# Three more pairs of dilated tiles as block products, and the places of the combinations handed on one by one

## The chip, the cores and the metric

The kernel runs on one core of one Trainium2 chip. The metric is the time of one execution on the device in microseconds (us); the runs of the kernel before are given by their median. The engines are called as in the profile: PE is TensorE (PEld its weight loads), DVE is VectorE, ACT is ScalarE, POOL is GpSimd, SP is SyncE. Each of them works through its own queue in order and waits on semaphores for the others; DMAs are issued from the queues of SP, ACT and POOL.

## The reference

One layer of a decoder on a sequence of 1024 tokens of width 1024, all in float32. Two kinds of attention run on the same normalised input, are gated and summed, and an FFN follows:

```python
h = rms_norm(x, norm_mix_g)
proj = h @ w_in                    # columns: dilated q, k, v (3 x 768), fox q, k, v (3 x 512), 8 fgt, 2 x 1024 gates
dil = proj[..., :o2].reshape(b, s, 3, 3, 4, 64)      # 3 groups of 4 heads
f_logit = proj[..., o3:o4] + b_fgt
gates = sigmoid(proj[..., o4:] + b_gate)
for g, (window, dilation) in enumerate(((128, 1), (512, 4), (2048, 16))):
    o_g, lse_g = dilated_window_attention(q_g, k_g, v_g, window, dilation, slopes[g])
o_a = sum over g of softmax(lse)_g * o_g
o_b = forgetting_attention(fox q, k, v, log_sigmoid(f_logit))   # causal, 8 heads, decay by the cumulated log f
x = x + (g_a * (o_a @ w_dil_out) + g_b * (o_b @ w_fox_out)) @ w_out
gu = rms_norm(x, norm_ffn_g) @ w_ffn_in
x = x + (silu(gu[..., :DFF]) * gu[..., DFF:]) @ w_ffn_down       # DFF = 2816
out = rms_norm(x, norm_final_g)
```

## The kernel before

Every float32 matrix is split into two float32r parts, hi (ACT, L96) and lo (DVE, L97), and a product is three matmuls, hi x hi, hi x lo, lo x hi (mm3, L100 to L102). h lies transposed in SBUF as hT, 128 partitions by 8 slices of the contraction by 1024 tokens. A "tile" below is 128 columns of w_in, so 128 rows of the transposed projection.

The order of the kernel is: norm and transposes, fox values; dilated values; the combinations T1 to T4 of h (form); projections of fox q and k and of some of the dilated q and k as block products; the attention, fox first and dilated behind it; the merges of both with their gates; w_out; the FFN. The order on each engine is found by a scheduler that runs a model of the machine when the kernel is built. It puts work without a near deadline in the gaps of other work.

There are two ways to project a tile, and the change is about them.

- ahead() computes one tile with 2 halves x 8 slices x 3 = 48 matmuls into two banks of PSUM of a pool of its own (psf, tiles pf). ACT evacuates each half into fst and issues its store. These calls are the fillers of the attention: the list BESIDE (eight dilated tiles) and, behind it in the text, sixteen tiles of the gates (GATE0).
- projections() computes a pair of tiles as a 2 x 2 block product with 7 products instead of 8 (prod, 4 slices x 3 = 12 matmuls each, 84 together). For that it needs sums of the blocks of h, T1 to T4, which live in SBUF, and sums of the blocks of the weights, which POOL makes for each pair (left_side, tiles s12 and s34). The banks are evacuated by copy (ACT) and join (DVE). Four pairs are fox q and k, and the two pairs of TWOS are dilated.

The outputs of a pair are two tiles qo of 128 x 1024, which POOL's queue stores whole once both halves are there; the fox ones (hl=True) go as hi and lo.

T1 to T4 lie in one tile of 64 KB per partition, in the pool comb1, which is closed after the last pair. The pools of the attention (beside with fst and the bias tables R0, R1, R2; attention with q, k, scores and values) are opened behind it over the same memory. Behind the attention, both are closed, and the pool gates of the merges lies over their memory: load_o loads the attention's output from DRAM into land, and splits it into oh and ol.

fox_qk loads q and k of a pair of heads from DRAM: kx (L570), qx (L570) and ql (L571), five DMAs for each of two heads, on ACT's queue. fox_scores makes the scores (L588 and L589), masks on POOL, takes the maximum over keys on DVE and then across partitions on POOL (partition_all_reduce, L603). fox_exp subtracts and exponentiates, fox_values multiplies by the values vf (L639), with the denominators in L642. finish divides. For the dilated heads dil_scores and dil_values do the same (L351, L778, L781).

Of the kernel before, what the change touches and what calls it, by code (L numbers as in the profile page):

```python
# [15 lines left out]
P = 128  # L16
# [31 lines left out]
def layer_kernel(  # L48
# [166 lines left out]

    def ahead(pool, c0, dst, dl=1, sc=1.0):
# [7 lines left out]
        for hh in range(2):  # L224
            st = pool.tile([P, dl, n], F32, tag="fst", name=nm("fst"), bufs=2)
            nc.scalar.activation(out=st[:], in_=view(pf[hh][:], dl), func=AF.Copy, scale=sc)  # L226
            nc.scalar.dma_start(out=dst.rearrange("p (r i) -> p r i", r=dl)[:, :, hh * n:(hh + 1) * n], in_=st[:])
# [5 lines left out]
    TWOS = [[(0, g, a) for g in range(2)] for a in range(2)]  # L233
    BESIDE = [(0, 2, 0), (0, 2, 1)] + [(1, g, a) for g in range(3) for a in range(2)]
# [19 lines left out]
    def left_side(pool, rg, ru, bufs):  # L254
# [9 lines left out]
        S34, A22, A1 = pair(KT, "s34", 1), pair(4, "a22", bufs), pair_of(rg[:])  # L264
# [16 lines left out]
    def projections(pool, T, c, dst, dls, sc, hl=False):  # L281

        T1, T2, T3, T4 = T
        o1, o2 = [pool.tile([P, dl, S // dl], F32, tag="qo", name=nm("qo"), bufs=3) for dl in dls]
        n1, n2 = [HALF // dl for dl in dls]
# [20 lines left out]
        copy(o1[:, :, :n1], b1, dls[0])  # L306
# [8 lines left out]
        for o, d in zip((o2, o1), dst[::-1]):  # L315
            flat = o[:].rearrange("p r i -> p (r i)")
            if hl:
                hi = pool.tile([P, S], F32R, tag="qh", name=nm("qh"), bufs=1)
                split(hi[:], flat, flat)
                nc.gpsimd.dma_start(out=d[0], in_=hi[:].bitcast(F32))  # L320
                nc.gpsimd.dma_start(out=d[1], in_=flat)
            else:
                nc.gpsimd.dma_start(out=d, in_=flat)
# [93 lines left out]
    with pool_of("comb1", 1) as tpool:  # L417
        hl = tpool.tile([P, 2, 4, 4, HALF], F32R, name="tT1")
        T1, T2, T3, T4 = T = [Pair(hl[:, 0, i], hl[:, 1, i]) for i in range(4)]

        def form(k0):
            ks = slice(k0, k0 + 2)
            f1, f2, f3, f4 = [wpool.tile([P, 2, HALF], F32, tag=t, name=nm("f"), bufs=2)
                              for t in ("wh", "wh", "wl", "wl")]

            def vec(out, p, q, op=ALU.subtract):
                nc.vector.tensor_tensor(out=out[:], in0=p[:], in1=q[:], op=op)

            def back(out, b):

                vec(out, b.hi[:, ks].bitcast(F32), b.lo[:, ks].bitcast(F32), ALU.add)

            def keep(t, f):
                split(t.hi[:, ks], t.lo[:, ks], f[:])

            back(f3, B11)
            back(f2, B12)
            back(f4, B22)
            vec(f1, f2, f3)
            keep(T1, f1)  # L440
            vec(f2, f4, f2)
            keep(T3, f2)
            vec(f4, f4, f1)
            keep(T2, f4)
            back(f3, B21)
            vec(f3, f3, f4)
            keep(T4, f3)
# [3 lines left out]
        with pool_of("dilv", 1) as vpool:  # L451
            sts = [vpool.tile([P, 512], F32, name=nm("vst"), bufs=1) for _ in range(2)]
            w12 = Pair(*[vpool.tile([P, KT, 512], F32R, name=nm("wv"), bufs=1) for _ in range(2)])
            last = load_wv(w12, [(2 * DIL_W + 256 + i * P, P, i * P) for i in range(4)])
# [15 lines left out]
            with tc.issue_after(last.ins):  # L470
                form(0)
                form(2)
# [628 lines left out]
```

## Time and profile before

| what | value |
|---|---|
| median of 3 runs | 1529.3 us (1529.08 to 1530.83) |
| the profiled execution | 1531.32 us, span 1529.5 us |
| PE busy | 1477.5 us, 97% |
| DVE busy | 888.2 us, 58% |
| ACT busy | 527.9 us, 35% |
| POOL busy | 410.9 us, 27% |
| mean granted clock of PE | 0.991 |
| HBM | 116 GB/s over the span |

The span runs from the first to the last instruction of the profiled execution. A row of instructions gives its start and its length in us, the engine (ACTq is a DMA issue on ACT's queue), the line of the kernel, the operation, output<-input, shapes and count; in square brackets stands how long the engine sat idle before it and what ended that. A row of waits reads "who <- for whom: us in total, times, longest". A row of a stretch of time gives its length and then, per engine, busy time and count, and behind them the granted clock of PE as a share of full speed, the busy share of the DMA engines and GB/s. A row of DMAs gives the queue, the count, KB of each and the median time from issue to landing.

### The profile page before, as it was taken

The page shows a single profiled execution, that of the slowest core. Times are in us where ns is not written, and L with a number is a line of the kernel's source. Part 1 is how long each engine was busy: PE and PEld are TensorE (multiplying, and loading weights), DVE is VectorE, ACT ScalarE, POOL GpSimd, SP SyncE. Part 2 cuts the span into 40 slices and gives each one's busy share as a digit, 9 for nine tenths or more (in the row PEclk, how much of TensorE's full clock was granted, in tenths as well). Part 3 has the DMA queues.
Part 4 walks back from the last instruction along what each step waited for, and adds up shares of the span by engine and source line. Part 5 has one row for each costly group of instructions (what it writes and reads, how often), then busy time and mean ns, then how long its engine had stood idle before and what let it go on. Part 6 is the DMA issues. An engine that isn't in the chain of part 4 may idle for free.

```text
span 1529.5 us, 18174 instructions
## 1 busy us (share of the span) xinstructions
PE 1477.5 (97%) x6956; PEld 1194.4 (78%) x6956; DVE 888.2 (58%) x1313; ACT 527.9 (35%) x800; POOL 410.9 (27%) x361
## 2 busy tenths in 40 slices
PE   7999999899999999989999999999999999999997
PEld 6898878676766676878888788888888877788886
DVE  6482544289899998126726863444444445956546
ACT  5242322266554332235414332222222224312113
POOL 1002232254332211000000055555555553140000
PEclk9999999999999999999999999999999999999999
DMA  8132434755443612436713122222222225642202
GB/s 255 46 93 62 135 127 152 213 130 132 117 110 126 220 49 83 145 107 189 268 55 138 42 69 83 84 83 83 83 83 83 83 91 188 202 152 83 96 15 96
DMA packets 154055, 177.92 MB, mean 116 GB/s; under 512 B 17904, under 2 KB 120304, under 8 KB 153968
## 3 DMA queue, kind: packets, MB, share of 16 engines
q1 hardware_dynamic: 115536, 97.56, 21.5%
q10 hardware_dynamic: 27632, 40.38, 8.7%
q0 software_dynamic: 10800, 38.81, 6.8%
q8 instruction: 55, 0.90, 0.2%
q14 instruction: 32, 0.26, 0.1%
HBM read 125.35 MB, written 51.38 MB: 116 GB/s over the span
## 4 chain that ended last, share of the span: by engine, by line
PE 77%; DVE 8%; DMA 6%; ACT 4%; POOL 3%; issue 2%; ACTq 0%; SPq 0%; DVEq 0%; POOLq 0%
PE pd L278 23%; PE pd L100 10%; PE pd L102 10%; PE pd L101 10%; PE pf L100 5%; PE pf L101 4%; PE pf L102 4%; DMA wr<-in_w_ffn_in_dram 3%; ACT wh L96 2%; PE pd L190 2%; PE pd L191 2%; PE pd L194 2%; DVE wl L97 2%; POOL sg L1009 1%; PE pd L639 1%
## 5 line engine op out<-in xcount | busy, mean ns | idle before, releaser
L97 DVE TENSOR_TENSOR wl<-wr,wh 128x1024 fp32r<-128x1024 f32 (+2 forms) x152 | 165.4, 1091 | 189.3 <-ACT wh L96 185.6
L96 ACT ACTIVATE wh<-wr 128x1024 fp32r<-128x1024 f32 (+2 forms) x152 | 140.8, 932 | 360.7 <-PE pd L101 89.3
L278 PE MATMUL pd<-hT_t,wh 128*128 128x512 f32 x784 | 242.0, 390 | 1.4 <-ACT cc L291 0.7
L278 PE MATMUL pd<-tT,wh 128*128 128x512 f32 x672 | 206.9, 392 | 2.1 <-ACT wh L96 1.5
L278 PEld LDWEIGHTS pd<-hT_t,wh 128*128 128x128 f32 x784 | 147.0, 188 | 32.3 <-ACT cc L291 1.1
L100 PE MATMUL pf<-hT_t,wh 128*128 128x512 f32 x384 | 153.1, 399 | 5.8 <-ACT fst L226 5.8
L278 PE MATMUL pd<-hT_t,wl 128*128 128x512 f32 x392 | 154.0, 393 | 1.7 <-DVE wl L97 1.4
L101 PE MATMUL pf<-hT_t,wh 128*128 128x512 f32 x384 | 152.9, 398 | 0.0
L102 PE MATMUL pf<-hT_t,wl 128*128 128x512 f32 x384 | 152.5, 397 | 0.0
L278 PEld LDWEIGHTS pd<-tT,wh 128*128 128x128 f32 x672 | 126.6, 189 | 30.0 <-ACT wh L96 2.9
L100 PE MATMUL pd<-wh,wh 128*128 128x512 f32 x352 | 137.3, 391 | 3.6 <-DVE acc L1052 2.3
L101 PE MATMUL pd<-wl,wh 128*128 128x512 f32 x352 | 137.0, 389 | 0.0
L102 PE MATMUL pd<-wh,wl 128*128 128x512 f32 x352 | 137.0, 389 | 0.0
L278 PE MATMUL pd<-tT,wl 128*128 128x512 f32 x336 | 130.7, 392 | 2.4 <-DVE wl L97 2.3
L266 POOL TENSOR_TENSOR s<-wr 128x512 f32<-128x512 f32 x26 | 37.6, 1446 | 339.4 <-DVE tT L97 195.6
L1052 DVE TENSOR_TENSOR acc<-pd,acc 128x512 f32<-128x512 f32 x128 | 85.4, 685 | 67.3 <-PE pd L102 67.2
L97 DVE TENSOR_TENSOR wl<-s,wh 128x1024 fp32r<-128x1024 f32 x52 | 67.0, 1289 | 63.8 <-ACT wh L96 60.8
L96 ACT ACTIVATE wh<-s 128x1024 fp32r<-128x1024 f32 x52 | 55.0, 1060 | 117.5 <-POOL s L267 93.7
L100 PEld LDWEIGHTS pf<-hT_t,wh 128*128 128x128 f32 x384 | 73.6, 192 | 25.1 <-ACT fst L226 6.6
L278 PEld LDWEIGHTS pd<-hT_t,wl 128*128 128x128 f32 x392 | 73.6, 188 | 22.5 <-DVE wl L97 7.4
L101 PEld LDWEIGHTS pf<-hT_t,wh 128*128 128x128 f32 x384 | 73.6, 192 | 18.4 <-issue 3.5
L102 PEld LDWEIGHTS pf<-hT_t,wl 128*128 128x128 f32 x384 | 73.2, 191 | 17.0 <-issue 1.8
(243 smaller groups left out, 2751.1 us busy)
## 6 DMA issues: line engine op xcount, KB each, us to landing
wr<-in_w_in_dram SPq DMA_DIRECT2D x46, 512.0 KB, 4.3
wr<-in_w_ffn_in_dram SPq DMA_DIRECT2D x44, 512.0 KB, 4.5
wr<-a_dram SPq DMA_DIRECT2D x22, 512.0 KB, 4.3
wr<-in_w_ffn_down_dram SPq DMA_DIRECT2D x22, 512.0 KB, 3.7
a_dram<-a POOLq DMA_DIRECT2D x20, 512.0 KB, 5.0
g_dram<-fst ACTq DMA_DIRECT2D x32, 256.0 KB, 2.1
land<-g_dram SPq DMA_DIRECT2D x16, 512.0 KB, 3.6
dqk<-dqk_dram ACTq DMA_DIRECT2D x12, 512.0 KB, 5.7
```

What stands on the lines that cost most here:

```text
L96: nc.scalar.activation(out=hi, in_=src, func=AF.Copy)
L97: return nc.vector.tensor_tensor(out=lo, in0=src, in1=hi.bitcast(F32), op=ALU.subtract)
L100: nc.tensor.matmul(psum, w.hi, m.hi, start=start, stop=False)
L101: nc.tensor.matmul(psum, w.hi, m.lo, start=False, stop=False)
L102: last_mm[0] = nc.tensor.matmul(psum, w.lo, m.hi, start=False, stop=stop)
L190: nc.tensor.matmul(pt[hh][:], w.hi[:, k], m.hi, start=(k == 0), stop=False)
L191: nc.tensor.matmul(pt[hh][:], w.hi[:, k], m.lo, start=False, stop=False)
L194: nc.tensor.matmul(pt[hh][:], w.lo[:, k], m.hi, start=False, stop=(k == kt - 1))
L266: nc.gpsimd.tensor_tensor(out=s12[:, :4], in0=u1, in1=u2, op=ALU.add)
L278: last_mm[0] = nc.tensor.matmul(bank[:], p, q, start=first and k == 0 and n == 0, stop=k == 3 and n == 2, skip_group_check=True)
L639: nc.tensor.matmul(po[half[e], HALF - width[j]:], vf[:, j, pr, e], L[:, off[j]:off[j + 1]], start=(j == nj - 1), stop=(j == 0), skip_group ...
L1052: nc.vector.tensor_tensor(out=acc[:, t, cs], in0=pt[:], in1=acc[:, t, cs], op=ALU.add)
```

## The change

1. TWOS gets three more pairs: tiles (u, g, a), with u the pair of heads, g the group, a = 0 for q and 1 for k. BESIDE shrinks from eight tiles to two.
2. projections() writes each half of an output tile as soon as it is evacuated (put), from four small qo tiles; stores of the dilated halves go to runs of 1024 / stride / 2 elements. For fox, the high halves are stored from ACT's queue.
3. T1 to T4 become eight tiles of 8 KB, place(0) to place(7), whose pool stays open through the attention. The attention puts its q, k, maxima, values and dilated score tiles into them, each free once the products that read it are done.
4. The loads of q and k of the first pair of heads go to POOL's queue instead of ACT's. The tables R0 to R2 and the clearing of ql's lower half follow these loads in the text; the clearing moves from POOL to DVE.
5. The pool beside is on the right side of SBUF and is closed only behind the merges.

The core of the diff:

```diff
-    TWOS = [[(0, g, a) for g in range(2)] for a in range(2)]
-    BESIDE = [(0, 2, 0), (0, 2, 1)] + [(1, g, a) for g in range(3) for a in range(2)]
+    TWOS = [[(0, g, a) for g in range(2)] for a in range(2)] + [[(0, 2, a), (1, 0, a)] for a in range(2)]
+    TWOS.append([(1, g, 0) for g in (1, 2)])
+    BESIDE = [(1, g, 1) for g in (1, 2)]
...
-        S34, A22, A1 = pair(KT, "s34", 1), pair(4, "a22", bufs), pair_of(rg[:])
+        S34, A22, A1 = pair(KT, "s34", 1), pair(4, "a22", 2), pair_of(rg[:])
...
+    def residues(d, r, hh):
+        n = HALF // r
+        return d.rearrange("p (r i) -> p r i", r=r)[:, :, hh * n:(hh + 1) * n]
...
-        o1, o2 = [pool.tile([P, dl, S // dl], F32, tag="qo", name=nm("qo"), bufs=3) for dl in dls]
+        def put(i, hh, op):
+            st = pool.tile([P, dls[i], HALF // dls[i]], F32, tag="qo", name=nm("qo"), bufs=4)
+            op(st[:], dls[i])
+            if hl:
+                flat = st[:].rearrange("p r i -> p (r i)")
+                hi = pool.tile([P, HALF], F32R, tag="qh", name=nm("qh"), bufs=2)
+                split(hi[:], flat, flat)
+                d = dst[i][:, :, hh * HALF:(hh + 1) * HALF]
+                nc.scalar.dma_start(out=d[0], in_=hi[:].bitcast(F32))
+                nc.gpsimd.dma_start(out=d[1], in_=flat)
+            else:
+                nc.gpsimd.dma_start(out=residues(dst[i], dls[i], hh), in_=st[:])
...
-        copy(o1[:, :, :n1], b1, dls[0])
+        put(0, 0, lambda o, r: copy(o, b1, r))
...
-        join(o2[:, :, n2:], b3, v3, dls[1])
+        put(1, 1, lambda o, r: join(o, b3, v3, r))
...
-        join(o2[:, :, :n2], b2, cc, dls[1])
+        put(1, 0, lambda o, r: join(o, b2, cc, r))
...
-        join(o1[:, :, n1:], b3, v2, dls[0])
+        put(0, 1, lambda o, r: join(o, b3, v2, r))
...
-        hl = tpool.tile([P, 2, 4, 4, HALF], F32R, name="tT1")
+    def place(n, name, dtype=F32R):
+        return tpool.tile([P, 2 * S], dtype, tag=f"T{n}", name=name, bufs=1)
+    T = [Pair(*[place(2 * n + i, nm("tT"))[:].rearrange("p (k c) -> p k c", k=4) for i in range(2)]) for n in range(4)]
...
+    qx, kx, ql = [[quarter(t, e) for e in range(2)] for t in (place(4, "qx"), place(5, "kx"), place(2, "ql"))]
+    mx, dl1, dl2 = [place(n, name, F32) for n, name in ((3, "mx"), (6, "dl1"), (7, "dl2"))]
+    v_half = [place(n, nm("v"), F32)[:] for n in range(2)]
...
-    f_ctx = pool_of("beside", 1)
+    f_ctx = pool_of("beside", 1, "right")
...
+            eng = nc.gpsimd if pr == 0 else nc.scalar
...
         for pr in range(4):
-            qk = fox_qk(apool, ql, pr)
+            fox_qk(pr)
+            if pr == 0:
+                for e in range(2):
+                    nc.vector.memset(ql[e][DH:].bitcast(F32), 0.0)
+                for i, t in enumerate(vf):
+                    nc.gpsimd.dma_start(out=t.rearrange("p t a b d -> p t (a b d)"),
+                                        in_=vf_dram[4 * i:4 * i + 4].rearrange("t p c -> p t c"))
+                tables()
```

What it does to the order of instructions is shown at three places. The rows are those of one engine's queue; names carry a running number, and in brackets stand the semaphores that a row waits for (DMAHW and DMASW are DMAs issued from SP or ACT, and from POOL).

First, the loads of q and k at the start of the attention. Before, they stand in ACT's queue ahead of the evacuation of pf_3264 into fst, on which PE's next filler waits:

```order
L226 ACTIVATE fst_3261<-pf_3203 128x512 [waits PE_49]
L227 DMA dqk_dram<-fst_3261 1024x1x64 [waits Activation_49]
L570 DMA kx_2055<-fqk_dram 64x1024 x2
L570 DMA qx_2053<-fqk_dram 64x1024 x2
L571 DMA ql_2049<-fqk_dram 64x1024 [waits DMAHW3_49]
L570 DMA kx_2056<-fqk_dram 64x1024 [waits DMAHW4_49]
...
L570 DMA qx_2054<-fqk_dram 64x1024 [waits DMAHW6_49]
...
L571 DMA ql_2050<-fqk_dram 64x1024 [waits DMAHW0_49]
L226 ACTIVATE fst_3320<-pf_3264 128x512 [waits PE_49]
```

Now they stand in POOL's queue, between the stores of the last two pairs (qo, to dqk_dram) and the first rows of the tables (dl and R) and of the masks (L):

```order
L303 DMA dqk_dram<-qo_2327 1024x1x64 [waits DMASW5_49,DVE_49]
L303 DMA dqk_dram<-qo_2400 512x1x128 [waits DMASW6_49,Activation_49]
L597 DMA kx<-fqk_dram 64x1024 [waits DMASW7_49,PE_49]
...
L597 DMA qx<-fqk_dram 64x1024 [waits DMASW3_49,PE_49]
...
L303 DMA dqk_dram<-qo_2428 1024x1x64 [waits DMASW7_49,DVE_49]
L567 IOTA dl_2467 128x256 [waits PE_49]
...
L303 DMA dqk_dram<-qo_2443 1024x1x64 [waits DMASW0_49,DVE_49]
L303 DMA dqk_dram<-qo_2458 512x1x128 [waits DMASW1_49,DVE_49]
L584 AFFINE_SELECT R_2477<-R_2477 128x512 [waits DVE_49]
L620 AFFINE_SELECT L_2516<-L_2516 128x128 [waits Activation_49]
```

There are four rows of kx and four of qx; the first of each waits for PE, the last reader of its place (T3). The ten loads left ACT, and POOL has three stores of joins behind them.

Second, PE at the same place. Before, the first scores (qx, kx) stand among fillers into pf:

```order
L101 MATMUL pf_3327<-hT_t,wh_3328 128x512
L588 MATMUL pd_2069<-qx_2053,kx_2055 128x512 [waits DMAHW2_49,DMAHW7_49,DMAHW1_49,DMAHW0_49]
L588 MATMUL pd_2077<-qx_2053,kx_2055 128x384
...
L589 MATMUL pd_2069<-ql_2049,kx_2055 128x512 [waits DMAHW3_49,Pool_49]
...
L588 MATMUL pd_2093<-qx_2053,kx_2055 128x256
...
L102 MATMUL pf_3327<-hT_t,wl_3329 128x512
```

Now they follow the last block product (pd_2361), and those of the second head (pd_2551) come eight rows later without a filler between:

```order
L284 MATMUL pd_2361<-hT_t,wl_2338 128x512
L613 MATMUL pd_2517<-qx,kx 128x512 [waits DMASW4_49,DMASW3_49,DMASW7_49,DMASW0_49,PE_49]
L614 MATMUL pd_2517<-ql,kx 128x512 [waits DMASW6_49]
L613 MATMUL pd_2525<-qx,kx 128x384 [waits PE_49]
...
L613 MATMUL pd_2541<-qx,kx 128x256 [waits Activation_49]
...
L613 MATMUL pd_2551<-qx,kx 128x512 [waits DMASW5_49,DMASW2_49,DMASW6_49,DMASW1_49,DVE_49]
```

The fillers that stood ahead of the first score and behind it have become block products further ahead.

Third, ACT behind the attention. Before, the splits of the fox output (oh) follow the store of the last gate tile (fst_5357) and wait for stores:

```order
L226 ACTIVATE fst_5354<-pf_5298 128x512 [waits DMAHW2_49,PE_49]
L227 DMA g_dram<-fst_5354 128x512 [waits Activation_49]
...
L226 ACTIVATE fst_5357<-pf_5299 128x512 [waits DMAHW3_49,PE_49]
L227 DMA g_dram<-fst_5357 128x512 [waits Activation_49]
L96 ACTIVATE oh_5364<-land_5366 128x1024 [waits DMAHW5_49,DMAHW6_49,DMASW7_49,DMASW6_49]
L96 ACTIVATE oh_5364<-land_5370 128x1024 [waits DMASW7_49]
```

Now all four stand ahead of the last gate tile's evacuations (fst_5377 and fst_5380), and wait for loads from POOL's queue alone:

```order
L232 DMA g_dram<-fst_5315 128x512 [waits Activation_49]
L96 ACTIVATE oh_5386<-land_5388 128x1024 [waits DMASW2_49,DMASW1_49]
...
L231 ACTIVATE fst_5318<-pf_5260 128x512 [waits DMAHW2_49,PE_49]
...
L96 ACTIVATE oh_5386<-land_5400 128x1024 [waits DMASW4_49]
...
L231 ACTIVATE fst_5377<-pf_5321 128x512 [waits DMAHW4_49,PE_49]
...
L96 ACTIVATE oh_5442<-land_5444 128x2x512 [waits DMASW5_49]
...
L96 ACTIVATE wh_5456<-wr_5458 128x512 [waits DMAHW3_49,PE_49]
L231 ACTIVATE fst_5380<-pf_5322 128x512 [waits DMAHW6_49,PE_49]
```

The splits moved ahead of the stores, and those of the dilated output (oh_5442) now stand ahead of the weights of the second merge (wh_5456). PE has 105 filler matmuls between the last denominators and the first merge, where it had 276.

More of the change, by code (lines that the diff above doesn't have):

```diff
@@ L558, in layer_kernel @@
[L558 to L565 removed]
+    t_ctx = pool_of("comb1", 1)
@@ new lines, in layer_kernel @@
+    with pool_of("proj", 1) as upool:
+        cums = [upool.tile([P] + d, F32, name=n, bufs=1) for n, d in (
+            ("sums", [2, P]), ("az", [NT * 8]), ("u", [NT * 8]), ("t1", [NT * 8]), ("tot", [NT, 8]))]
+        for pr in range(0, 4, 2):
+            for a in range(2):
+                c0 = FOX0 + a * FOX_W + pr * P
+                projections(upool, T, (c0, c0 + P), [fqk_dram[a, pr + i] for i in range(2)], (1, 1),
+                            (SCALE, 1.0)[a], True)
+            if pr == 0:
+                decay(*cums)
+        for two in TWOS:
+            projections(upool, T, [dil_cols(*t) for t in two], [dqk_dram[t] for t in two],
+                        [STR[a][g] for u, g, a in two], (SCALE, 1.0)[two[0][2]])
@@ L795, in layer_kernel @@
         for u in range(2):
[L796 removed]
+            qk = dil_qk(u)
             for b in range(2):
```

295 lines of the change are left out of this document (133 added, 162 removed).

## The prediction

> **What bounds the kernel now.** I read the page first, then the stages between landmarks of the trace, then what TensorE (PE) waited for, then the other engines around those waits.
>
> ```profile
> PE 1477.5 (97%) x6956; PEld 1194.4 (78%) x6956; DVE 888.2 (58%) x1313; ACT 527.9 (35%) x800; POOL 410.9 (27%) x361
> PE 77%; DVE 8%; DMA 6%; ACT 4%; POOL 3%; issue 2%; ACTq 0%; SPq 0%; DVEq 0%; POOLq 0%
> ```
>
> PE is busy for 97% of the span and is 77% of the chain that ended last. So a matmul taken away counts in full wherever PE sets the pace, and what else can be won is PE's idle time and the time in which its clock is held down. The stages (columns: stretch, length, then busy time and count of PE, weight loads, DVE, ACT, POOL, granted clock, DMA share, GB/s) are the projections up to the first score product, the attention, the gate projections left after it, and the rest:
>
> ```profile
> 138.07:300.00 161.93, 151.45 (x644) 122.44 (x642) 72.33 (x87) 43.32 (x54) 51.43 (x56) 0.97 0.50 154
> 300.00:612.00 312.00, 302.78 (x1687) 220.67 (x1685) 275.45 (x473) 154.04 (x278) 99.73 (x102) 0.98 0.42 120
> 612.00:679.40 67.40, 62.98 (x278) 51.75 (x277) 8.41 (x10) 14.37 (x22) 2.66 (x5) 1.00 0.34 113
> 679.40:1529.50 850.10, 833.53 (x3664) 681.08 (x3664) 458.70 (x632) 267.48 (x363) 248.16 (x178) 1.00 0.33 108
> ```
>
> The change ends at the second merge; from there the order of all engines is that of before, so the last row only shifts. PE sat idle for 24 us in the three other rows, 10 us of it in two waits:
>
> ```profile
> PE pf L100 <- ACT fst L226: 5.8, 1, 5.8
> PE pd L190 <- ACT oh L96: 4.4, 1, 4.4
> PE pd L781 <- DVE Mx L740: 4.0, 3, 1.6
> PE pd L278 <- DVE wl L97: 2.3, 2, 1.2
> ```
> ```profile
> 280.00:300.00 20.00, 14.20 (x52) 11.20 (x50) 1.23 (x1) 2.03 (x3) 0.00 (x0) 0.83 0.96 244
> 680.00:700.00 20.00, 20.00 (x83) 16.22 (x82) 11.42 (x14) 13.51 (x14) 1.06 (x2) 0.92 0.70 233
> 505.00:612.00 107.00, 98.80 (x659) 72.86 (x657) 96.23 (x156) 34.00 (x51) 13.78 (x10) 0.95 0.34 115
> ```
>
> Each of the two long waits also costs clock: 20 x (1 - 0.83) = 3.4 us behind the first, 20 x (1 - 0.92) = 1.6 us behind the second. So the first wait costs 9.2 us in all and the second 6.0 us. The first is ACT standing in front of its own DMA issues: it loads q and k for the attention, and the evacuation that frees a bank for PE is queued behind ten of these. The second is a matter of memory, seen on ACT:
>
> ```profile
> 675.91 0.33 ACTq L227 DMA_DIRECT2D g_dram<-fst  x1
> 678.26 3.90 ACT L96 ACTIVATE oh<-land 128x1024 fp32r<-128x1024 f32 x4 [2.39 <-DMA g_dram<-fst]
> ```
>
> The split of the attention's output (oh) waits for the store of the last gate projection, since its tiles lie where the pool "beside" with fst lay. The outputs themselves had been sent for at 616.7 (row below) and landed some 50 us earlier.
>
> **The change, part by part.** The pace of a 512-column matmul in a full stretch of gate projections:
>
> ```profile
> 615.00:670.00 55.00, 55.00 (x244) 45.56 (x243) 6.33 (x11) 1.00 0.37 125
> ```
>
> 55.00 / 244 = 0.226 us. A pair of tiles through ahead() is 2 x 48 matmuls, through projections() 7 products of 12, so 84. Three pairs save 36 matmuls: 36 x 0.226 = -8.1 us. The order says where: ahead of the first score product stand 806 instead of 640 matmuls, in the attention 711 instead of 742 fillers, behind it 105 instead of 276.
>
> The attention does not give back all of its 31 fillers. Its parts:
>
> ```profile
> 300.00:326.00 26.00, 26.00 (x127) 21.68 (x127) 16.09 (x34) 18.30 (x37) 11.82 (x16) 1.00 0.48 121
> 326.00:505.00 179.00, 177.98 (x907) 126.13 (x904) 163.12 (x285) 101.75 (x192) 74.14 (x77) 1.00 0.45 122
> ```
>
> From 326 to 505 PE is full and DVE has 16 us of slack: the 6 fillers that leave it count. From 505 (row above) DVE is busy for 96 of 107 us and PE already waits for it; 7 fillers less there, 1.6 us, I cost as not gained. In the first unit (300 to 326) 18 leave, 4.1 us. Its other chain is nearly as long:
>
> ```profile
> 300.00 0.68 PE L588 MATMUL pd<-qx,kx 128*128 128x512 f32 x3
> 310.44 1.80 POOL L603 PARTITION_ALL_REDUCE Mx<-Mx  x1 [6.97 <-issue]
> 318.58 1.77 POOL L603 PARTITION_ALL_REDUCE Mx<-Mx  x1
> 323.27 0.61 ACT L622 ACTIVATE L<-L 128x256 f32<-128x256 f32 x2
> 325.77 1.52 PE L639 MATMUL pd<-L,vf 128*64 128x128 f32 x12
> ```
>
> The exponentials are done at 323.9, 1.9 us ahead of the values, so the chain takes about 23.9 us against PE's 25.8 - 4.1 = 21.7. The tables of the dilated bias now stand in that unit on POOL, seven instructions (first and last shown, 3.4 us together) that ran under the projections before (the memset of the third row is used below):
>
> ```profile
> 267.55 0.35 POOL L530 IOTA ri<- 128x256 int32 x1 [15.74 <-PE pd L278]
> 272.01 0.64 POOL L552 TENSOR_SCALAR_AFFINE_SELECT R<-R 128x512 f32<-128x512 f32 x1
> 273.57 1.84 POOL L650 MEMSET ql<- 64x1024 f32 x2
> ```
>
> They delay the first reduction, but its 6.97 us start-up is the same, and the scores now come closer together. I take 24.7 us for the unit: 1 of the 4.1 us is gained. Bounds: all 4.1 gained, or a unit 3.4 us longer than PE's old 25.8. Not gained in the attention: 3.1 + 1.6 = +4.7 us.
>
> The wait at 282 goes, -9.2 us, since the first loads of q and k leave ACT's queue. What is late next is these loads themselves. They now go out on POOL behind the last reader of T3, and the order leaves 41 matmuls between that reader and the first score: 9.3 us. POOL issues four loads in 2.25 us, and they land in 5.6 us:
>
> ```profile
> 616.68 2.25 POOL L835 DMA_DIRECT2D land<-o_dram  x4 [0.24 <-issue]
> land<-o_dram POOLq DMA_DIRECT2D x6, 512.0 KB, 5.6
> 274.68 12.83 DMA kx<-fqk_dram
> ```
>
> The sixth of the eight loads (all kx first, then qx) is enough for head 0: 6 x 0.56 + 5.6 = 9.0 us; the eighth, for head 1, 10.1. Wait of 0 to 1 us; I take +1. At worst a load takes the 12.8 us that one took on the chain of before: 3.4 + 12.8 - 9.3 = 6.9 us, with clock behind it. I take the lower, since these loads are the nearest in queue and the vf load that shared that moment now goes out 16 us earlier, behind T1's last reader. ql's memset moves to DVE, 1.84 us in a stage where DVE is busy 72 of 162 us; if that cover went, they would show.
>
> Three more pairs run in a stage whose weights arrive just in time:
>
> ```profile
> 185.98 3.73 DMA wr<-in_w_in_dram
> 192.71 2.28 POOL s L267
> 196.10 2.34 DVE wl L97
> ```
> ```profile
> 196.12 1.19 PE L278 MATMUL pd<-tT,wh 128*128 128x512 f32 x4 [0.39 <-ACT wh L96]
> 198.48 0.69 PE L278 MATMUL pd<-tT,wl 128*128 128x512 f32 x1 [1.17 <-DVE wl L97]
> 220.94 0.50 PE L278 MATMUL pd<-tT,wl 128*128 128x512 f32 x1 [1.18 <-DVE wl L97]
> ```
>
> Load, sums on POOL, split: past the start, two of the six pairs stalled, by 0.39 + 1.17 and by 1.18 us. The mean over the four pairs that follow the first two is 0.7 us; three more at that: +2 us; bounds 0 and 3 x 1.56 = 4.7. The stores by halves put twenty instead of four stores to dqk_dram on POOL's queue, each waiting for a join, with the sums of a later pair queued behind; and sixteen stores of the high halves move to ACT. POOL is busy 51 and ACT 43 of 162 us there, so I cost both at nothing; without that cover each store would cost its issue, 0.3 to 0.6 us (rows of L227 and L835).
>
> The stores also come in shorter pieces, 64 elements where the stride is 8. The trace has both kinds, 256 KB each:
>
> ```profile
> g_dram<-fst ACTq DMA_DIRECT2D x32, 256.0 KB, 2.1
> dqk_dram<-fst ACTq DMA_DIRECT2D x16, 256.0 KB, 4.2
> ```
>
> The short pieces land 2.1 us later, and a fox stage of 179 us (row above) passes until they are read. The Trainium skill, "DMA: Bandwidth & Descriptors", Specifications, asks for at least 512 B a piece and says that shorter ones cost a read-modify-write; the pair of rows agrees in direction. By that rule the last four stores would slow the q and k loads that follow them, which is the first rival's mechanism.
>
> The wait at 675 goes: "beside" now lies on the right and is closed behind the merges, so the split has only the attention's end ahead of it. The order has 105 fillers left there, 105 x 0.226 = 23.8 us. Needed, by the rows of before:
>
> ```profile
> 611.10 1.02 PE L781 MATMUL pd<-Mx,ones 128*64 128x512 f32 x3
> 614.91 0.69 DVE L342 SCALAR_TENSOR_TENSOR o<-pd,den 128x512 f32<-128x512 f32 x1
> over<-vd_dram POOLq DMA_DIRECT2D x1, 1024.0 KB, 14.0
> ```
>
> From the end of the denominators, 612.1, to the first load at 616.7 are 4.6 us, landing 5.6, split 1: 11.2 us. The two dilated outputs reuse the same landing tiles, some 9 us later with their splits on ACT at 21 to 23; the second merge needs ACT behind them at 23.8 + 24 x 0.226 = 29.2. Term: -6.0 us.
>
> Sum: -8.1 + 4.7 - 9.2 + 1 + 2 - 6.0 = -15.6 us. The profiled execution took 1531.3 us (span 1529.5); against it 1515.7. It is 2.0 above the median of the runs, 1529.3, and on that footing the result is 1513.7, forecast as 1514.
>
> On clock: in 505 to 612 no single gap is over 2.2 us, yet the clock there is 0.95. The Trainium skill, "TensorE: Matmul & The Clock Gate", HAM oscillation, sets the limit at gaps above about 3.4 us; the 5.8 and 4.4 us gaps agree, this row does not. By the rule a 1 to 3 us wait at the first score costs no clock and the sum stands; by the row it can cost 1.7 us more, which the range takes in.
>
> **Rivals.** (1) Late loads: the q and k loads take the 12.8 us of the chain's row, and the place of the old gap is taken by a new one of 6.9 us with 1.7 to 3.4 us of clock. For it: DMA share 0.96 in 280 to 300. Against: half of that traffic has moved away. 1513.7 - 1 + 6.9 + 2.5 = 1522. (2) The gap ahead of the merges stays, since the cover behind the attention shrinks from 61 to 24 us and the output's loads now end last: a landing of 14 us (the slowest POOL load, row of over) still fits for the first merge, but not for the dilated outputs in front of ACT's next weights; 4 to 6 us, 1519. (3) Slower: the block stage turns from PE's pace to that of its chain, weights, sums on POOL, split, with POOL held by stores that wait for joins. It has to eat 15.6 + 3.1 us, 2.1 us for each of nine pairs beyond forecast; at 2.5 us a pair the time is 1536. For it: POOL runs in order and got sixteen more waiting stores. Against: the worst pair so far lost 1.6 us, and the last two none. (4) More is gained: the first unit gives its 4.1 us, no pair stalls: 1513.7 - 3.1 - 2 - 1 = 1507.6.
>
> **Chances and range.** Forecast, 1508 to 1520 with (2) in its milder form: 0.70. (1), or (1) and (2) in part, 1520 to 1526: 0.16. (4) and beyond: 0.06. (3): 0.05. No change within 0.2% (3.1 us, about what this measurement can tell): 0.03. So faster 0.92, same 0.03, slower 0.05. The range 1507 to 1524 leaves out the ends of (1), all of (3) and what lies beyond (4).
>
> **What would show it.** Right: six tiles (288 matmuls) fewer into pf and 252 more from the block products; no gap near 282 with ACT as releaser; first score near 331 us, last values near 641; oh's split within the fillers, PE without a gap of 2 us ahead of L190, merges from about 665. Wrong: PE waiting for kx or qx loads by more than 3 us; gaps of over 2 us per pair with wl or wh as releaser; an attention longer than 312 us. What would break the forecast most is a POOL queue that holds the sums behind stores.

## The result, and the profile after

The changed kernel takes 1508.54 us in the median (1507.19 to 1510.32, four runs) against 1530.07 us for the kernel before beside it: a ratio of 0.986, 95% interval 0.9843 to 0.9877. That is 21.5 us less, where 15.6 were forecast; 1508.5 lies inside the range and below the forecast of 1514. The profiled execution took 1507.19 us with a span of 1505.5. One run of one kernel below (1651.75 us, clock 0.847) fell into a slower state and is left out of that kernel's median.

The page of the changed kernel, engines and chain of waits:

```profile
PE 1463.1 (97%) x6920; PEld 1183.9 (79%) x6920; DVE 910.7 (60%) x1344; ACT 530.6 (35%) x808; POOL 440.8 (29%) x398
PE 84%; DVE 7%; DMA 3%; ACT 2%; issue 2%; POOL 2%; ACTq 0%; SPq 0%; DVEq 0%; POOLq 0%
```

TensorE's share of the chain went from 77 to 84%, and the DMAs' from 6 to 3%. That is no measure of the gain: 3 of the 6% were the loads of the FFN's weights, which the change doesn't touch. The stages between the same landmarks as before (length, PE, weight loads, DVE, ACT, POOL, granted clock, DMA share, GB/s), in order the projections, the attention, the rest of the gate tiles, and everything behind:

```profile
138.60:325.85 187.25, 183.93 (x810) 150.72 (x808) 99.05 (x118) 56.34 (x75) 80.01 (x87) 1.00 0.51 152
325.85:635.10 309.25, 297.33 (x1656) 214.69 (x1656) 276.29 (x478) 151.10 (x275) 102.23 (x108) 0.98 0.41 119
635.10:659.00 23.90, 23.90 (x106) 19.74 (x107) 9.01 (x10) 12.54 (x15) 3.71 (x7) 1.00 0.74 244
659.00:1505.50 846.50, 831.08 (x3665) 680.13 (x3663) 453.06 (x629) 262.00 (x359) 246.92 (x176) 1.00 0.33 107
```

The projections grew by 25.3 us and hold 166 matmuls more, the attention shrank by 2.8, the stretch behind it from 67.4 to 23.9, and the merges now start at 659 in place of 679. The last row is 3.6 us shorter: 1.7 of it is the clock that the old gap cost, and 2 us lie in an FFN whose code did not change (the profiled execution before was 1.3 us above its median, this one 1.3 below). The longest of what TensorE still waits for between 130 and 700, and two shorter waits:

```profile
PE pd L809 <- DVE mx L768: 5.7, 3, 3.0
PE pd L613 <- ACT L L617: 2.7, 1, 2.7
...
PE pd L284 <- ACT wh L96: 1.0, 1, 1.0
PE pd L613 <- DMA qx<-fqk_dram: 1.0, 1, 1.0
```

The waits for fst (5.8), for oh (4.4) and for wl (2.3) are gone. No block product waits but two at the start of the stage (wh, 1.0, and cc, 0.8), as before (1.1 and 0.7); the new wait for q is 1.0 us as forecast, and one of 2.7 us is new in the first unit of the attention.

### The profile page after: what moved, and what is told of

Its sections match the earlier page's. It is cut to its first block, busy times and chain, and to the rows that moved or that the text cites. A ratio compares the mean times of both kernels' runs of the same rounds, so it can differ in the third digit from the quotient of the medians.

```text
span 1505.5 us, 18223 instructions
## 1 busy us (share of the span) xinstructions
PE 1463.1 (97%) x6920; PEld 1183.9 (79%) x6920; DVE 910.7 (60%) x1344; ACT 530.6 (35%) x808; POOL 440.8 (29%) x398
## 4 chain that ended last, share of the span: by engine, by line
PE 84%; DVE 7%; DMA 3%; ACT 2%; issue 2%; POOL 2%; ACTq 0%; SPq 0%; DVEq 0%; POOLq 0%
PE pd L284 33%; PE pd L100 10%; PE pd L102 10%; PE pd L101 10%; PE pf L100 3%; PE pf L101 3%; PE pf L102 3%; PE pd L190 2%; PE pd L194 2%; PE pd L191 2%; PE pd L664 2%; PE pd L613 1%; PE pd L614 1%; DMA wr<-in_w_in_dram 1%; DVE mx L766 1%
## 5 line engine op out<-in xcount | busy, mean ns | idle before, releaser
L284 PE MATMUL pd<-hT_t,wh 128*128 128x512 f32 x856 | 264.4, 390 | 1.5 <-ACT cc L310 0.8
L284 PE MATMUL pd<-tT,wh 128*128 128x512 f32 x768 | 236.3, 389 | 2.2 <-DVE v L952 1.1
L284 PEld LDWEIGHTS pd<-tT,wh 128*128 128x128 f32 x768 | 144.0, 188 | 32.9 <-DVE v L952 1.6
L284 PE MATMUL pd<-hT_t,wl 128*128 128x512 f32 x428 | 168.0, 393 | 0.2 <-DVE wl L97 0.2
L272 POOL TENSOR_TENSOR s<-wr 128x512 f32<-128x512 f32 x29 | 41.3, 1426 | 371.5 <-DVE tT L97 203.2
L284 PE MATMUL pd<-tT,wl 128*128 128x512 f32 x384 | 148.5, 390 | 0.1
L100 PE MATMUL pf<-hT_t,wh 128*128 128x512 f32 x288 | 114.3, 397 | 0.4 <-ACT wh L96 0.4
L101 PE MATMUL pf<-hT_t,wh 128*128 128x512 f32 x288 | 114.2, 397 | 0.0
L102 PE MATMUL pf<-hT_t,wl 128*128 128x512 f32 x288 | 113.6, 395 | 0.0
L284 PEld LDWEIGHTS pd<-tT,wl 128*128 128x128 f32 x384 | 72.1, 188 | 15.4 <-DVE wl L97 0.5
L100 PEld LDWEIGHTS pd<-wh,wh 128*128 128x128 f32 x352 | 66.1, 188 | 19.6 <-DVE acc L1080 2.9
L102 PE MATMUL pd<-wh,hT_t 128*128 128x512 f32 (+1 forms) x208 | 79.1, 382 | 0.0
```

Source lines behind the costliest of these rows:

```text
L100: nc.tensor.matmul(psum, w.hi, m.hi, start=start, stop=False)
L101: nc.tensor.matmul(psum, w.hi, m.lo, start=False, stop=False)
L102: last_mm[0] = nc.tensor.matmul(psum, w.lo, m.hi, start=False, stop=stop)
L272: nc.gpsimd.tensor_tensor(out=s12[:, :4], in0=u1, in1=u2, op=ALU.add)
L284: last_mm[0] = nc.tensor.matmul(bank[:], p, q, start=first and k == 0 and n == 0, stop=k == 3 and n == 2, skip_group_check=True)
```

## The experiments

The times are medians; beside them stands the kernel before on the same chip, 1529.5 to 1530.2 us in all comparisons, so that kernels of different comparisons can be set against each other to about 2 us. A total holds more than the edit, though. The part from the first merge on, where most of these edits change nothing, takes 846.5 us in the trace of the changed kernel, 850.2 in that of the kernel before, and up to 854.3 in the others with the same matmuls there; and the scheduler moves fillers with every edit. Where a few us decide, the stage is read and not the total.

**The three pairs alone, and all the rest without them.** The kernel before with the new lists, and the changed kernel with the old ones:

```diff
-    TWOS = [[(0, g, a) for g in range(2)] for a in range(2)]
-    BESIDE = [(0, 2, 0), (0, 2, 1)] + [(1, g, a) for g in range(3) for a in range(2)]
+    TWOS = [[(0, g, a) for g in range(2)] for a in range(2)] + [[(0, 2, a), (1, 0, a)] for a in range(2)]
+    TWOS.append([(1, g, 0) for g in (1, 2)])
+    BESIDE = [(1, g, 1) for g in (1, 2)]
```

> The kernel before with the three more pairs alone: eight loads of q and k on ACT's queue, whole outputs and the old memory stay. Theory: the 36 matmuls saved (8.1 us) are not gained, since the fillers run out. 60 fewer are left in the last unit of the attention, where DVE sets the pace (some 7 us not gained), the wait near the first score (5.8 us) and the one ahead of the merges (4.4 us) stay, and the pairs add stalls of 0.7 us each: 0 to 6 us slower than before. Rival, matmuls count in full wherever they go: 8.1 us faster.

> The changed kernel with the old lists of tiles: two dilated pairs as block products and eight tiles as fillers; outputs by halves, places and loads on POOL's queue stay. Theory: most of the gain is here. The wait behind the q and k loads goes (9.2 us with its clock), the gap ahead of the merges goes (6.0), the stalls near 196, 199 and 220 us go since POOL makes its sums in the order in which PE needs them (about 3 to 4), and 1 us of a new wait for q and k comes: 15 to 18 us faster, so that the three pairs on top are worth 4 to 7 of their 8.1 us. Rival: freed memory is only what the three pairs need, and gains little by itself: 0 to 8 us faster.

The pairs alone: 1537.05 against 1530.15, ratio 1.0049 (1.0035 to 1.0063), 7 us slower. The rest alone: 1513.17, ratio 0.9894 (0.9879 to 0.991), 17 us faster. So 36 matmuls fewer cost time on the old memory, and on the new one the pairs bring 4.6 us of the 8.1 that they were counted at. The waits of the pairs alone, from 640 to 700:

```profile
PE pd L779 <- ACT over L755: 7.9, 2, 4.1
PE pd L190 <- ACT oh L96: 5.6, 1, 5.6
PE pd L782 <- DVE Mx L741: 3.0, 2, 1.6
```

With only 15 fillers left in the last unit of the attention (75 in the kernel before), TensorE waits there for DVE and ACT, and the gap ahead of the merges stays. The theory held; the price was over its upper bound by 1 us.

**One pair more.** The changed kernel with a fourth pair, so that BESIDE is empty:

```diff
-    TWOS.append([(1, g, 0) for g in (1, 2)])
-    BESIDE = [(1, g, 1) for g in (1, 2)]
+    TWOS += [[(1, g, a) for g in (1, 2)] for a in range(2)]
+    BESIDE = []
```

> The changed kernel with a fourth pair more (the last two tiles of BESIDE), so that only the sixteen gate tiles are fillers: 12 matmuls fewer, 2.7 us. Theory: the fillers run out: 3 are left in the last unit of the attention in place of 77, and 48 behind it in place of 105, so PE waits for DVE and then for the outputs' loads: 3 to 13 us slower than the changed kernel. Rival, matmuls count in full: 2.7 us faster.

1517.22, ratio 0.9923 (0.9906 to 0.9939): 8.7 us slower than the changed kernel with 12 matmuls fewer. Its waits from 620 on, and the clock there:

```profile
PE pd L806 <- ACT over L782: 11.1, 2, 8.3
```
```profile
630.00:650.00 20.00, 8.86 (x72) 5.32 (x71) 16.43 (x26) 7.33 (x11) 5.00 (x3) 0.66 0.13 41
```

So the fillers last for three pairs and not for four; one or two pairs on the new memory were not run. DVE is busy for 16 of these 20 us: with no filler in the last dilated unit, TensorE waits for it.

**The wait at 282: whose is it?** The prediction put it down to ACT standing in front of its own issues. Three kernels test that: the changed one with its first loads on ACT's queue again, the one before with them on POOL's queue, and the one before with them on ACT's queue but the 2 MB load of vf sent later.

```diff
# changed kernel
-            eng = nc.gpsimd if pr == 0 else nc.scalar
+            eng = nc.scalar
# kernel before, loads on POOL's queue
-                        nc.scalar.dma_start(out=to[e][half[i], :].bitcast(F32), in_=src[i])
-                nc.scalar.dma_start(out=ql[e][:DH, :].bitcast(F32), in_=q[1])
+                        eng.dma_start(out=to[e][half[i], :].bitcast(F32), in_=src[i])
+                eng.dma_start(out=ql[e][:DH, :].bitcast(F32), in_=q[1])
# kernel before, vf later: its load is taken from the head of the attention to here
+                if not pend:
+                    with tc.issue_after(first_mask[0].ins):
+                        nc.gpsimd.dma_start(out=vf[:].rearrange("p t a b d -> p t (a b d)"),
+                                            in_=vf_dram.rearrange("t p c -> p t c"))
```

> The changed kernel with the first loads of q and k on ACT's queue, as before; places and pairs stay. Theory of the prediction: ACT stands in front of ten DMA issues and the evacuations behind them come late, so the wait near the first score returns, 3 to 9 us slower than the changed kernel. Rival: the wait of before came from the memory, which let the loads start only behind the last block product; with places freed one by one ACT issues them early enough and PE loses under 1 us.

> The kernel before with the first ten loads of q and k on POOL's queue in place of ACT's, nothing else. Theory of the prediction, ACT's evacuations stood behind these issues: the wait of 5.8 us at 282 goes with its 3.4 us of clock, 6 to 9 us faster than before. Rival, the wait belongs to the traffic of that moment (the 2 MB of vf, the stores in short pieces, weights, and these loads at a DMA share of 0.96), whichever queue sends it: PE then waits for weights or for the loads themselves, 0 to 3 us faster.

> The kernel before with the 2 MB load of vf sent only behind the first mask of the attention; the loads of q and k stay on ACT's queue. Theory: ACT's ten issues took 13.9 us in place of about 6 because their transfers queued behind vf and the short stores; without vf they take 6 to 8 us, and the wait at 282 shrinks to under 2 us: 5 to 9 us faster than before, less up to 2 us if vf is then late for the first values. Rival, ten issues in front of an evacuation are enough by themselves: the wait stays, within 2 us of before.

Loads on ACT in the changed kernel: 1508.24, ratio 0.9865 (0.9845 to 0.9885), the same as the changed kernel. Loads on POOL in the kernel before: 1531.63 against 1529.54, ratio 1.0014 (1.0003 to 1.0025), no faster at all. vf later: 1523.33, ratio 0.9958 (0.9946 to 0.9971), 6.2 us faster. So the queue alone is not the cause. ACT's queue in the kernel before, in the changed kernel with loads on ACT, and in the one with vf later:

```profile
273.95 2.14 ACTq L570 DMA_DIRECT2D kx<-fqk_dram  x2
276.12 3.31 ACTq L570 DMA_DIRECT2D qx<-fqk_dram  x2
...
280.12 5.63 ACTq L570 DMA_DIRECT2D kx<-fqk_dram  x2
```
```profile
316.85 1.11 ACTq L597 DMA_DIRECT2D kx<-fqk_dram  x2
318.05 1.20 ACTq L597 DMA_DIRECT2D qx<-fqk_dram  x2
```
```profile
272.89 1.34 ACTq L570 DMA_DIRECT2D kx<-fqk_dram  x2
...
279.81 1.11 ACTq L570 DMA_DIRECT2D qx<-fqk_dram  x2
```

In the kernel before the ten issues took 14.0 us (273.95 to 287.98), with vf later 8.7. A row of two holds the time between them as well. Taken one by one, three issues of the kernel before last 1.3 to 2.0 us, the others 0.5 to 0.7, and 4.6 us are a pause:

```profile
277.43 2.00 ACTq L570 DMA_DIRECT2D qx<-fqk_dram  x1
...
280.12 0.61 ACTq L570 DMA_DIRECT2D kx<-fqk_dram  x1
285.30 0.45 ACTq L570 DMA_DIRECT2D kx<-fqk_dram  x1
```

The load at 285.30 uses the semaphore of an earlier DMA, the store of fst sent at 273.39, and waits for that one: it goes out 0.02 us after the store landed, at 285.28. The store had left 0.8 us behind vf and took 11.9 us; with vf later, the same store took 3.2 us, no issue lasted over 0.74, and TensorE did not wait for fst at all. With the loads on POOL's queue ACT no longer stands, and TensorE waits longer than before; its wait, what ACT waited for, how long the five stores of fst from 260 to 300 took to land, and the stretch:

```profile
PE pf L100 <- ACT fst L226: 8.8, 1, 8.8
```
```profile
272.18 0.54 ACTq L227 DMA_DIRECT2D dqk_dram<-fst  x1
...
295.27 0.60 ACT L226 ACTIVATE fst<-pf 128x512 f32<-128x512 f32 x1 [12.72 <-DMA dqk_dram<-fst]
```
```profile
DMA to landing us min/median/max: 2.0/3.0/23.0
```
```profile
280.00:300.00 20.00, 11.20 (x42) 8.87 (x41) 1.23 (x1) 2.26 (x3) 1.55 (x3) 0.74 0.96 234
```

fst has two buffers, so the evacuation at 295.27 needs that of the store sent at 272.18, which landed after 23.0 us, where the median of the five is 3.0. The wait is one of traffic: vf, ten loads, two weights and the short stores of the fillers at once, at a DMA share of 0.96 by either queue. Sending vf later is enough to end it: from the first block product to the first score that kernel took 144.5 us with 38 matmuls fewer (8.6 us), where the kernel before took 162.1, so 9.0 us are gained there. The changed kernel has vf apart as well, as two loads sent for at 297 that have landed by 307; its loads go out at 315.6, and no store of a filler until 330. Its level time with the loads on ACT does not mean that the queue is free: there TensorE waits 3.6 us for q and k in place of 1.0, and the scheduler placed the fillers otherwise (24 of them behind the start of the first merge). What that kernel shows is that the wait for fst stays away (0.6 us).

**The gap ahead of the merges.** The changed kernel with the split of the fox output lying over fst again:

```diff
+    f_ctx.__exit__(None, None, None)
+    oh_ctx = pool_of("ohright", 1, "right")
+    ohpool = oh_ctx.__enter__()
...
-            o = Pair(mpool.tile([P, n, S], F32R, name=nm("oh"), bufs=1),
+            o = Pair((ohpool if br else mpool).tile([P, n, S], F32R, name=nm("oh"), bufs=1),
```

> The changed kernel, with one thing put back: the split of the fox output (oh) lies over fst again, so that it waits for the last stores of the gate tiles; the order and number of matmuls are the same. Theory: the gap ahead of the first merge comes back, 4.4 us and 1.6 us of clock, since the split is the last thing that the merge waits for: 4 to 6 us slower than the changed kernel. Rival: with only 105 fillers behind the attention, the loads of the outputs end last anyway, or another evacuation hides it: under 1 us.

1516.53, ratio 0.9914 (0.9899 to 0.993), 8.0 us slower than the changed kernel. Its wait, its split on ACT, and the clock:

```profile
PE pd L190 <- ACT oh L96: 4.5, 1, 4.5
```
```profile
659.77 3.90 ACT L96 ACTIVATE oh<-land 128x1024 fp32r<-128x1024 f32 x4 [2.45 <-DMA g_dram<-fst]
```
```profile
660.00:680.00 20.00, 18.92 (x71) 15.06 (x72) 10.77 (x12) 13.41 (x14) 1.06 (x2) 0.85 0.65 216
```

The same gap as in the kernel before, with the same releaser. By the trace's record of the clock TensorE's clock is at half speed from 659.31 to 666.14; the wait ends at 660.88, so 5.3 us of work run at half speed and 2.6 us are lost: 7.1 us in all, where the gap and its clock cost 6.1 in the kernel before. The mechanism is as told. That the total rose by 8.0 is not all the gap's: in the traces the attention is 3.4 us shorter than in the changed kernel, and the part behind the merge start, without those 2.6 us, 4.8 longer; no run shows why.

**Why no pair stalls.** Two things differ in the block products: a22 has two buffers, and POOL makes its sums in another order. The order isn't in the diff, it is the scheduler's. In the kernel before, all six pairs have their sums crossed, s34's first ahead of s12's second; in the changed kernel only the first two of nine have, and the others have them in turn. Four kernels look at this. First the order alone, put in turn in the kernel before, and crossed in the changed one:

```diff
# kernel before: s34's first sum behind s12's second
+        with tc.issue_after(s12b.ins):
+            nc.gpsimd.tensor_tensor(out=s34[:, :4], in0=g1, in1=u1, op=ALU.subtract)
# changed kernel: s12's second sum behind s34's first
+        with tc.issue_after(s34a.ins):
+            nc.gpsimd.tensor_tensor(out=s12[:, 4:], in0=s12[:, :4], in1=g1, op=ALU.subtract)
```

> The kernel before, where POOL now makes the first sum for s34 only behind the second sum for s12, as in the changed kernel; nothing else differs, and PE has the same order. Theory: the stalls of 0.39, 1.17 and 1.18 us in the block products, and the 1.7 us of clock at 198, came from this order alone: 3 to 4.4 us faster. Rival, they came from POOL's whole stores or from late loads of weights: no difference (under 1 us).

> The changed kernel, where POOL makes the first sum for s34 ahead of the second sum for s12 in all nine pairs, as the kernel before did in most of its six. Theory: the stalls on wh and wl in the block products come back, 1 to 1.6 us in some pairs and a drop of clock: 3 to 6 us slower than the changed kernel. Rival, the chain of the weights has slack by the halves and the smaller stores: under 1 us slower.

In turn: 1526.54 against 1530.15, ratio 0.9981 (0.9972 to 0.999), 3 us faster by the ratio and 3.6 by the medians. Of the waits for wl, 1.2 and 1.2 us, two of 0.5 and 0.6 us are left, at 217 and 237:

```profile
PE pd L279 <- DVE wl L97: 1.1, 2, 0.6
```

The price is as told: the stalls are 1.6 us less, and the 1.7 us of clock at 198 are gone. But the order alone does not take every stall away. Crossed: 1517.93, ratio 0.9922 (0.9909 to 0.9936), 9.4 us slower, but not where it was expected. The projections are only 0.5 us longer, with one stall; the loss lies in the FFN, whose block products use the same function and had the order in turn in the changed kernel for all but their first two pairs. The stall in the projections, and the waits of the FFN from 880 to 1240:

```profile
PE pd L285 <- DVE wl L97: 0.7, 1, 0.7
```
```profile
PE pd L285 <- ACT wh L96: 8.2, 11, 1.5
```

In the projections of the changed kernel the order costs next to nothing, so something else had made room there. Next the buffer: one in the changed kernel, two in the one before.

```diff
# changed kernel
-        S34, A22, A1 = pair(KT, "s34", 1), pair(4, "a22", 2), pair_of(rg[:])
+        S34, A22, A1 = pair(KT, "s34", 1), pair(4, "a22", bufs), pair_of(rg[:])
# kernel before
-        S34, A22, A1 = pair(KT, "s34", 1), pair(4, "a22", bufs), pair_of(rg[:])
+        S34, A22, A1 = pair(KT, "s34", 1), pair(4, "a22", 2), pair_of(rg[:])
-        ... name=nm("qo"), bufs=3) for dl in dls]
+        ... name=nm("qo"), bufs=2) for dl in dls]
```

> The changed kernel with one buffer for a22 in place of two (the scheduler then leaves 58 fillers behind the attention in place of 105). Theory: what took the old stalls away is this buffer. With it the split that reads a pair's raw weights last need not wait for the product of the pair before, both raw buffers come free together, and the loads of the next pair go out some 10 us earlier (172.7 and 175.0 in the changed kernel, 177.4 and 186.0 in the one before). With one buffer the loads are 10 us apart again and the nine pairs stall by about 0.7 us each: 4 to 8 us slower than the changed kernel. Rival, the order of the sums on POOL alone took them away: under 2 us slower.

> The kernel before with two buffers for a22; to make room, its whole outputs qo have two buffers in place of three. Theory: the weights' loads come early, the stalls near 196, 197 and 220 us and the dropped clock behind them go: 3 to 5 us faster than before, less what the missing output buffer costs. Rival, the buffer does nothing: no difference, or slower by the missing output buffer.

One in the changed kernel: 1511.23, ratio 0.9872 (0.9856 to 0.9889), 2.7 us slower, between theory and rival, and not resolved from the changed kernel by the intervals. Two in the kernel before: 1523.58 against 1529.54, ratio 0.9957 (0.9944 to 0.9969), 6 us faster, more than expected and with an output buffer less. How the weights are sent for shows in SP's queue; the second number is the time from the first issue to the end of the second. The kernel before, that kernel with two buffers, the changed kernel, and the changed kernel with one:

```profile
177.37 8.98 SPq L245 DMA_DIRECT2D wr<-in_w_in_dram  x2
```
```profile
170.85 2.60 SPq L245 DMA_DIRECT2D wr<-in_w_in_dram  x2
```
```profile
172.73 2.60 SPq L251 DMA_DIRECT2D wr<-in_w_in_dram  x2
```
```profile
177.82 10.17 SPq L251 DMA_DIRECT2D wr<-in_w_in_dram  x2
```

With one buffer the second load of a pair ends 9 to 10 us after the first is sent; by the code, the split that reads a raw buffer last must wait for the product of the pair before. With two they go together. In the kernel before with two buffers, no block product waits between 150 and 320. In the changed kernel with one, five wait, briefly:

```profile
PE pd L284 <- DVE wl L97: 2.0, 4, 0.6
PE pd L284 <- ACT wh L96: 0.4, 1, 0.4
```

But the buffer moves the order too. POOL's sums of one pair in the changed kernel (L272 and L273 are s12's, L276 and L277 s34's), and with one buffer:

```profile
180.05 1.29 POOL L272 TENSOR_TENSOR s<-wr 128x512 f32<-128x512 f32 x1 [4.62 <-DVE v L315]
181.42 1.29 POOL L273 TENSOR_TENSOR s<-s,wr 128x512 f32<-128x512 f32 x1
...
191.08 1.66 POOL L276 TENSOR_TENSOR s<-wr,wr 128x512 f32<-128x512 f32 x1 [2.50 <-DVE wl L97]
```
```profile
192.34 1.28 POOL L272 TENSOR_TENSOR s<-wr 128x512 f32<-128x512 f32 x1 [3.12 <-DMA wr<-in_w_in_dram]
193.58 1.30 POOL L276 TENSOR_TENSOR s<-wr,wr 128x512 f32<-128x512 f32 x1
194.84 1.28 POOL L273 TENSOR_TENSOR s<-s,wr 128x512 f32<-128x512 f32 x1
```

With one buffer all nine pairs are crossed; with two in the kernel before, four of its six are in turn. So these two kernels change buffer and order together, and only with the two above do the six traces tell them apart. The stalls of block products from 150 us to the first score, in all:

| loads of a pair | sums crossed | sums in turn |
|---|---|---|
| apart | 2.7 us (before), 2.4 (changed, one buffer) | 1.1 (before, in turn) |
| together | 0.7 (changed, crossed) | 0 (changed; before, two buffers) |

Each of the two takes most of the stalls away, and together they take all. Of the 6 us of the kernel before with two buffers, part is the wait at 282, which shrank from 5.8 to 4.0 us: there vf is sent 3 us ahead of the ten loads, an issue lasts 0.5 to 0.7 us, and ACT waits only with the last two and with the store behind them, for the first three loads to land.

None of these kernels is faster than the changed one; the loads on ACT's queue are level with it.

## Why the prediction was right, point by point

- *The end of the wait at 282, -9.2 us.* The gain came, the reason was wrong, and that is luck. The step that failed is "since the first loads of q and k leave ACT's queue": that alone gained nothing, and the wait stays away with the loads left on ACT. What the runs showed in its place is the meeting of vf, the loads, and the fillers' stores; the change moved vf as well, which the prediction had noted only for the new wait. It put ACT's standing down to the ten issues as such, where 4.6 of the 14.0 us were a pause until a store had landed, and three issues were long. The size was a little over: the clock of 0.83 counts 1.3 us in which TensorE still stood, so the clock cost 2.8 us and not 3.4, and the whole 8.6.
- *The gap ahead of the merges, -6.0 us.* Right in place, mechanism and landmark: 23.9 us from the last denominators to the merges, 23.8 forecast (105 x 0.226 is 23.7). The first split starts at 647.5, 12.4 us behind the denominators, where 10.2 were worked out. Putting the memory back cost 7.1 us at that place.
- *Three more pairs, -8.1 and +2 us for stalls.* The matmuls count as told. The stalls term is the one that was mis-sized: the added pairs stalled by nothing, and the old stalls went as well (2.7 us and 1.7 of clock at 198), together 6.4 us better than +2. The prediction passed over the line of the diff that did it, a22's second buffer, which by itself takes these stalls out of the kernel before, by earlier loads and by the order of the sums that comes with them. It is the main reason for a first score at 325.9 and not at 331.
- *The attention, +4.7 us not gained of 7.0.* Right in sum: it shrank by 2.8 us, forecast 2.3. Its parts differ: the first unit gained nothing (26.0 us, forecast 24.7, with a new wait of 2.7 us), and the stretch behind it gained the rest. The unit's length isn't fixed by the change: it took 23.8 us with oh over fst, where it has the same fillers. Why, no run shows.
- *The new wait for q and k, +1 us.* 1.0 us. The sixth load landed 10.0 us after the first was sent (315.60 to 325.60), where 9.0 were worked out.
- *The short pieces.* The row of 4.2 us doesn't show what they cost: of its sixteen stores of dqk_dram only ten have pieces of 256 B, and four have 2 KB. In quieter moments one of 256 B took 3.0 us (268.13) and one of 2 KB 2.6 (303.25). The term was put at nothing, and no run shows one.
- *Rivals.* Late loads (1) and the gap that stays (2) did not come. Of (3), the chain of the weights, the opposite happened in the projections; the fear was not idle, as the FFN with crossed sums shows, at 8.2 us. (4) named the time, 1507.6, and half its reason (no pair stalls); the first unit it named did not gain.

The sum with measured terms: -8.1 for the matmuls, -4.4 for the stalls, -8.6 + 1.0 at the first score, +4.2 not gained in the attention, -6.1 ahead of the merges: -22.0 us, against 22.1 between the traces at the merges (20.4 in their start, 1.7 in clock).

## What to carry to other kernels

A wait behind an engine's DMA issues may belong to the traffic and not to the queue: take the row of issues apart, see whether an issue lasts long or waits for an earlier DMA to land, and look at how long that one took, before moving loads to another queue. A buffer count that looks like bookkeeping sets when the next loads leave, and can turn the scheduler's order as well; follow the last reader of each raw buffer, and compare the order before naming the buffer as the cause. Work that is saved counts only as long as enough fillers are left where another engine sets the pace: the same 36 matmuls, counted at 8.1 us, gained 4.6 on the new memory and cost 7 on the old.

## What the runs showed of the hardware that was not expected

In these traces the clock that a gap costs does not grow with the gap. A low granted clock costs nothing while TensorE stands idle, and part of the half speed falls there. The wait at 282 of the kernel before, and the end of the one with the loads on POOL's queue, cut where the record of the clock changes and where TensorE goes on (the DMA share is rough in stretches as short as these):

```profile
282.88:287.36 4.48, 0.00 (x0) 0.00 (x0) 0.00 (x0) 0.00 (x0) 0.00 (x0) 1.00 1.09 273
287.36:288.68 1.32, 0.00 (x1) 0.00 (x1) 0.00 (x0) 0.65 (x2) 0.00 (x0) 0.50 1.04 239
288.68:294.19 5.51, 5.51 (x13) 4.36 (x14) 1.23 (x1) 1.38 (x2) 0.00 (x0) 0.50 1.03 231
```
```profile
289.55:295.92 6.37, 0.00 (x0) 0.00 (x0) 0.00 (x0) 0.60 (x1) 0.00 (x0) 0.50 1.06 251
295.92:299.79 3.87, 3.87 (x9) 3.13 (x10) 0.00 (x0) 0.60 (x1) 0.00 (x0) 0.50 0.55 155
```

Of the time in which TensorE works at half speed, half is lost: 2.8 us behind the wait of 5.8, and 1.9 behind the one of 8.8. Counted in the same way, a gap of 4.0 us cost 1.7 (two buffers for a22), one of 4.4 cost 1.7 (kernel before, 675), one of 4.5 cost 2.6 (oh over fst), and one of 8.3 with one of 2.8 close behind cost 2.0 (fourth pair). The product of a stretch's length and its missing clock, 20 x (1 - 0.74) = 5.2 us for the wait of 8.8, says too much. And a gap of 2.7 us was enough in the changed kernel:

```profile
340.00:360.00 20.00, 17.35 (x78) 12.58 (x79) 18.69 (x35) 14.08 (x29) 12.29 (x14) 0.91 0.82 185
```

In the trace's records of the clock, each of these stretches runs at half speed for 3.4 us or a multiple of it (6.8, 10.2, 13.7), idle time included. The limit of about 3.4 us for a single gap, in the Trainium skill, "TensorE: Matmul & The Clock Gate", HAM oscillation, does not hold in the row above. The section gives about 1.67 us of throttled time to each gap of its case; here the shortest stretch at half speed is 3.4 us, twice that.
